# Mixers of a two-block model on one core: weight splits on VectorE, both base inverses in one pass, band attention paced anew, heads in the array's halves

## The chip, the cores and the metric

The kernel runs on one core of one Trainium2 chip, in one launch. The metric is the device time of the run in microseconds (us), the median of a few runs. The engines are TensorE (PE, with PEld for its weight loads), VectorE (DVE), ScalarE (ACT), GpSimd (POOL) and SyncE (SP), which here only issues transfers.

## The reference

Two blocks follow each other over 512 tokens of width 1024, all in float32. The first block has two layers, each a token mixing (a pooling branch, sparse attention with an index that picks 128 keys, memory attention) and a mixture of 16 experts. The second block is what the change is about: feed-forward, mixers, feed-forward.

```
proj = rms_norm(x) @ w_in                 # 1024 -> 3600
qkv_a, z_a, a_a, b_a, qkv_b = split(proj)
o_a = gdn_mixer(qkv_a, z_a, a_a, b_a)     # 4 heads of 128
o_b = dilated_mixer(qkv_b)                # 8 heads of 64
x = x + concat(o_a, o_b) @ w_out
```

`gdn_mixer` convolves q, k and v over five tokens, applies silu, normalises q and k, and runs a gated delta rule over the tokens in both directions: per block a lower (or upper) triangular system is solved (`tmat = inverse(1 + lmat)`), and a scan carries a state of 128x128 per head from block to block. `dilated_mixer` is softmax attention under a band mask with relative bias; its three dilations are merged in the kernel into one softmax whose bias has the logarithm of the number of patterns that hold a pair.

## The kernel before, in words

Everything on TensorE that is a dense product runs in three passes (`mm3`, `feat`, `tok`): each operand is split into a high half rounded to fp32r and the low rest, and high by high, high by low and low by high are summed. Smaller products run as plain fp32, which the trace shows as two records for each.

Weights come through one stream (`Stream`). `load` issues the transfers on SP's queue, `split` makes the high half on ScalarE (L182) and the low half by a subtraction (L185) on VectorE, or on GpSimd for the units that `plan` marks as slow; `SLOWP` marks ten of the twelve input panels of the mixers, 20 units. There are five staging places (`turn` takes the next); a panel gives its places back when it is done.

The order of the work is written out by a small planner. `Kern.now` is a clock of its own in nanoseconds. Dense products advance it by `adv`, and within the mixers' later part (`count`) every `mm` advances it by 214 or 4n/2.4 ns. Side tasks are generators that yield how long they want to pause; `run_tasks` and `drive` step the task that is due. All queues then run in the order so written. `pipeline` runs a list of items through stages with lags and pauses `gap` between: 4300 for the layers' attention, `self.gap` for the band attention.

The mixers (`mixers`) go as follows.

- Input panels: twelve panels `ga0..5` (for the delta rule, by `feat`) and `sq0..5` (for the band, by `tok`). Beside them run `conv` (five taps on VectorE at L1896 and L1898, tanh on ScalarE, transposes at L1915 and L1945, norms), `normed` (norms of the band's q and k, transposes at L1817), `gates` (decay sums, L1979 to L2013), `gdn_couples` (four couples of blocks: the strict triangle, stored to DRAM as `nd`, pauses `CP`), and `gdn_base` (the inverses of all 16x16 diagonal blocks by 15 steps of row updates on VectorE, L2092 and L2093, for one direction and then the other; stored to DRAM as `td`).
- `gdn_builds`: `load` fetches `dct` (8 transfers), `nd` (8) and `C` from `td` (4 for each direction) on SP's queue; `attend` makes the decayed products; three lanes of `invert` grow the 16x16 inverses to 128x128 with 64-column products. GpSimd spreads the base (L2172).
- `gdn_scan`: two chains, one for each direction, of four steps; then `close` and the output projection (`project`).
- `band_attention`: 32 items (8 heads by 4 query blocks) from the end of the panels on, interleaved with builds and scan by the planner; what is left runs after the scan. An item has a score (one fp32 product of 64 rows by 512 columns into a bank of tag `sa`), a softmax (L909 to L913), four transposes into a bank of tag `tp` (L864), a copy (L866), four value products over all 128 columns of a pair's values, of which the head's 64 are copied out (L1864).

The layers' sparse attention (`dsa`) uses the same `attention`; its scores already run in pairs: `pair` puts the two heads of a pair into the upper and lower 64 rows of the array, three fp32r passes each, from a query split by `halves`.

Of the kernel before, what the change touches and what calls it, by code (L numbers as in the profile page):

```python
# [18 lines left out]
NT = S // 128  # L19
# [213 lines left out]
class Kern:  # L233
# [218 lines left out]
    def plan(self):  # L452
# [49 lines left out]
        for j, (n, i) in enumerate(PANELS):  # L502
            c = (0 if n == "ga" else 2064) + i * 256
            ws.plan((n, i), W[:, c:c + 256], 8, 256, j in SLOWP)
# [287 lines left out]
    def halves(self, q):  # L792

        a = self.m1.tile([128, 2, 128], F32R, name="qs", tag="bt", bufs=2)
        self.split(a[:, 0], a[:, 1], q)
        return a

    def pair(self, q, kH, kL):
# [4 lines left out]
        for i, (a, b) in enumerate(((0, kH), (0, kL), (1, kH))):  # L803
            for r in range(2):
                c = slice(r * 64, r * 64 + 64)
                self.mm(ps[r], q[c, a, :], b[c], i == 0, i == 2)
        return ps

# [44 lines left out]
    def attention(self, pool, scores, v, add, width, out, tag="sa"):  # L853

        nc = self.nc

        def first(st, qb, h):
            st["P"] = self.softmax(scores(qb, h), add(qb, h), width(qb), pool)
# [19 lines left out]
    def dsa(self, qT, kH, kL, v, sc, oT, done):  # L878
# [3 lines left out]
        held, ready = {}, {}  # L882

        def split(i):
            if i < len(pairs):
                qb, pr = pairs[i]
                ready[i] = self.halves(qT[:, pr, qb * 128:(qb + 1) * 128])

        def scores(qb, h):
            if h % 2:  # L890
                split(qb * 4 + h // 2 + 1)
                return held.pop(h)
            pr, W = h // 2, (qb + 1) * 128
            ps, held[h + 1] = self.pair(ready.pop(qb * 4 + pr), kH[:, pr, :W], kL[pr // 2][:, pr % 2, :W])
            return ps

        def out(r, pr, c, po):
            self.split(oH[r, pr, c], oL[r, pr, c], po)
        split(0)
# [780 lines left out]
    def mixers(self, xT, close):  # L1680
# [13 lines left out]
        with ExitStack() as left:  # L1694
            pool = lambda n: left.enter_context(tc.tile_pool(name=n, bufs=1, reuse_waits="tile"))
            sw = pool("sw")
            qkv = [sw.tile([128, 4, S], F32, name=n) for n in ("sqT", "skT")]
            qkv.append(sw.tile([128, NT, 512], F32, name="sv"))
            with tc.tile_pool(name="cw", bufs=1, reuse_waits="tile", side="right") as cw:
                with tc.tile_pool(name="pn", bufs=1, reuse_waits="tile") as self.pn:  # L1700
                    self.za_panel(xT, 1)
                    tasks = [self.side(self.gates()), self.side(self.zgates())]
# [6 lines left out]
                with tc.tile_pool(name="bw", bufs=1, reuse_waits="tile", side="right") as self.bw:  # L1709
                    self.gap = G1  # L1710
# [8 lines left out]
            self.drive(lambda: att in self.tasks)  # L1719
        pool = lambda n: self.left.enter_context(tc.tile_pool(name=n, bufs=1, reuse_waits="tile"))  # L1720
# [68 lines left out]
    def windows(self, xT, qT, kT, v):  # L1789
# [8 lines left out]
        def normed(raw, dst, col):  # L1798
# [15 lines left out]
            for j in range(2):  # L1814
# [3 lines left out]
                nc.scalar.activation(dst[:, j, :], p, AF.Copy, scale=col)  # L1818
                yield 600

        def panel(i):
# [8 lines left out]
            if i < 4:  # L1830
                d = (qT if i < 2 else kT)[:, 2 * (i % 2):2 * (i % 2) + 2, :]
# [16 lines left out]
    def band_attention(self, at, qT, kT, v, oB):  # L1848
# [3 lines left out]
        def bias(h):  # L1852
            if h < 8:
                E[h] = at.tile([128, 896], F32, name="E", tag="E", bufs=2)
# [3 lines left out]
        def add(qb, h):  # L1858
            if qb == 0:
                bias(h + 1)  # L1860
            return E[h][:, 384 - 128 * qb:896 - 128 * qb]

        def out(r, pr, c, po):
            nc.vector.tensor_copy(oB[r, pr, c], po)  # L1864

        bias(0)
        def scores(qb, h):
            p0, pr = (h % 2) * 64, h // 2
            ps = self.psum("sa")
            self.mm(ps, qT[p0:p0 + 64, pr, qb * 128:(qb + 1) * 128], kT[p0:p0 + 64, pr, :], True, True)  # L1870
            return ps
        stages = self.attention(at, scores, v, add, lambda qb: 512, out)
        yield from self.pipeline([(qb, h) for h in range(8) for qb in range(NT)], stages, None)

    def gdn_in(self, xT):
# [6 lines left out]
        def conv(i, pss):  # L1882
# [138 lines left out]
    def gdn_couples(self, p):  # L2021
# [5 lines left out]
        bnd = p.tile([128, 2, 128], F32, name="bndN")  # L2027
# [42 lines left out]
        for d in range(2):  # L2070
            yield from self.gdn_base(p, d)
            self.based.append(d)

    def gdn_base(self, p, d):

        nc, V = self.nc, self.nc.vector
        B = p.tile([128, 16, 16], F32, name="B", tag="B")
        X = p.tile([128, 2, 16, 16], F32, name="X", tag="X")
        tmp = p.tile([128, 64], F32, name="Bt", tag="Bt")
        nc.sync.dma_start(B, bass.AP(tensor=self.nd.tensor, offset=self.nd.offset + d * 128 * STEP,  # L2080
                                     ap=[[STEP, 128], [128, 16], [1, 16]]))
        T = X[:, 0]
        Tf = T.rearrange("p r c -> p (r c)")
        nc.gpsimd.memset(Tf, 0.0)
        nc.gpsimd.memset(Tf[:, ::17], 1.0)
        yield 4000
        for k in range(15):
            j = 15 - k if d else k
            rows, cols = (slice(0, j), slice(j, 16)) if d else (slice(j + 1, 16), slice(0, j + 1))
            sh = [128, 15 - k, k + 1]  # L2090
            x = tmp[:, :sh[1] * sh[2]].rearrange("p (a b) -> p a b", b=sh[2])
# [287 lines left out]
```

## Time and profile before

| | us |
|---|---|
| median of 3 runs (lowest, highest) | 3046.87 (3046.29, 3047.41) |
| profiled execution, whole time | 3070.84 |
| its span, first to last instruction | 3069.1 |
| PE busy, PEld busy | 2840.8 (93%), 2274.0 (74%) |
| DVE, ACT, POOL busy | 1933.7 (63%), 1281.1 (42%), 495.7 (16%) |
| mean granted TensorE clock | 0.955 |

The profile is of one execution, and times within it count from the span's first instruction. Busy TensorE time is modelled and counts slow clock as busy; the granted clock is a share of full speed. A row with "[x <-engine tile line]" gives idle time before it and what ended that.

### The profile page before, as it was taken

What the parts mean: (1) busy time and instruction counts of PE and PEld (TensorE: products, weight loads), DVE (VectorE), ACT (ScalarE), POOL (GpSimd) and SP (SyncE); (2) the same over time, 40 slices, a digit from 0 to 9 for tenths busy, and PEclk for the clock granted to TensorE, in tenths of its full rate; (3) what the DMA queues carried; (4) which work ended last, traced back from release to release, by engine and by line L of the source; (5) the groups of instructions that cost most, each with busy time, mean ns of one, the idle gap of its engine ahead of it and who ended that gap; (6) DMA issues with size and microseconds to landing.
All of it is one profiled execution on the core that took longest, in us unless ns stands there. A gap on an engine that the chain in (4) does not pass through costs nothing. (4 is left out here: it accounts for less than half of the span.)

```text
span 3069.1 us, 38719 instructions
## 1 busy us (share of the span) xinstructions
PE 2840.8 (93%) x14283; PEld 2274.0 (74%) x14283; DVE 1933.7 (63%) x3555; ACT 1281.1 (42%) x2077; POOL 495.7 (16%) x546
## 2 busy tenths in 40 slices
PE   7989999999989898998899979999988698999998
PEld 7767778876757676876667757888877586787877
DVE  5677544798986876437799973333578546444244
ACT  3533432377864433422678832222334222323132
POOL 1000002264120000111551110000155121010000
PEclk9999989999989999998899989999999798999999
DMA  6212215899963122228799924323323401123231
GB/s 195 86 55 82 67 56 175 307 357 351 346 237 107 45 76 65 76 76 322 255 353 352 323 64 145 110 82 100 112 83 105 113 20 37 51 90 108 85 102 70
DMA packets 295586, 448.27 MB, mean 146 GB/s; under 512 B 30402, under 2 KB 155986, under 8 KB 294880
## 3 DMA queue, kind: packets, MB, share of 16 engines
q1 hardware_dynamic: 274816, 382.66, 37.8%
q0 software_dynamic: 20000, 60.99, 6.2%
q8 instruction: 114, 1.87, 0.2%
q10 hardware_dynamic: 576, 2.10, 0.2%
q14 instruction: 80, 0.66, 0.1%
HBM read 423.02 MB, written 34.65 MB: 149 GB/s over the span
## 5 line engine op out<-in xcount | busy, mean ns | idle before, releaser
L185 DVE TENSOR_TENSOR wL<-wR,wH 128x1024 fp32r<-128x1024 f32 (+2 forms) x361 | 445.1, 1256 | 259.5 <-ACT wH L182 257.2
L294 PE MATMUL mm<-xTH,wH 128*128 128x512 f32 (+1 forms) x1376 | 541.4, 393 | 0.3 <-ACT xTH L351 0.2
L294 PE MATMUL mm<-xTH,wL 128*128 128x512 f32 (+1 forms) x1376 | 531.2, 386 | 7.7 <-DVE wL L185 7.7
L294 PE MATMUL mm<-xTL,wH 128*128 128x512 f32 (+1 forms) x1376 | 529.6, 385 | 2.5 <-DVE xTL L352 2.5
L182 ACT CAST wH<-wR 128x1024 fp32r<-128x1024 f32 (+1 forms) x394 | 399.9, 1042 | 260.4 <-PE mm L294 222.3
L294 PEld LDWEIGHTS mm<-xTH,wL 128*128 128x128 f32 x1376 | 262.8, 191 | 66.5 <-DVE wL L185 15.1
L294 PEld LDWEIGHTS mm<-xTH,wH 128*128 128x128 f32 x1376 | 263.7, 192 | 55.0 <-issue 4.7
L294 PEld LDWEIGHTS mm<-xTL,wH 128*128 128x128 f32 x1376 | 263.6, 192 | 49.5 <-DVE xTL L352 3.2
L294 PE MATMUL mm<-wH,hH 128*128 128x512 f32 (+1 forms) x608 | 241.0, 396 | 0.0
L294 PE MATMUL mm<-wH,hL 128*128 128x512 f32 (+1 forms) x608 | 239.1, 393 | 0.6 <-DVE hL L352 0.6
L294 PE MATMUL mm<-wL,hH 128*128 128x512 f32 (+1 forms) x608 | 238.6, 392 | 0.0
L294 PE MATMUL mm<-wH,xTH 128*128 128x256 f32 (+3 forms) x576 | 203.6, 353 | 11.9 <-DVE rx L754 5.3
L294 PE MATMUL mm<-wH,gH 128*96 128x512 f32 x512 | 206.3, 403 | 0.0
L294 PE MATMUL mm<-wH,gL 128*96 128x512 f32 x512 | 203.6, 398 | 0.0
L294 PE MATMUL mm<-wL,gH 128*96 128x512 f32 x512 | 202.4, 395 | 0.0
L294 PE MATMUL mm<-wH,xTL 128*128 128x256 f32 (+3 forms) x576 | 190.6, 331 | 3.6 <-DVE xTL L352 3.6
L294 PE MATMUL mm<-wL,xTH 128*128 128x256 f32 (+3 forms) x576 | 190.1, 330 | 0.0
L185 DVE TENSOR_TENSOR wL<-wX,wH 128x1024 fp32r<-128x1024 f32 x142 | 169.2, 1222 | 7.3 <-ACT wH L182 6.9
L182 ACT CAST wH<-wX 128x1024 fp32r<-128x1024 f32 x142 | 145.3, 1049 | 9.6 <-PE mm L294 8.9
L1647 DVE TENSOR_TENSOR th<-th,mm 128x512 f32<-128x512 f32 x44 | 30.2, 687 | 168.8 <-PE mm L294 168.8
L294 PEld LDWEIGHTS mm<-wH,hL 128*128 128x128 f32 (+1 forms) x608 | 107.3, 177 | 34.0 <-DVE hL L352 1.4
L294 PEld LDWEIGHTS mm<-wH,xTH 128*128 128x128 f32 x576 | 113.4, 197 | 25.0 <-DVE rx L754 6.2
(529 smaller groups left out, 5316.2 us busy)
## 6 DMA issues: line engine op xcount, KB each, us to landing
wX<-in_w SPq DMA_DIRECT2D x141, 512.0 KB, 11.3
wR<-in_w_in SPq DMA_DIRECT2D x116, 512.0 KB, 3.7
wR<-in_w SPq DMA_DIRECT2D x73, 512.0 KB, 11.4
wY<-in_w SPq DMA_DIRECT2D x69, 512.0 KB, 10.7
X<-in_w SPq DMA_DIRECT2D x56, 512.0 KB, 11.9
wZ<-in_w SPq DMA_DIRECT2D x45, 512.0 KB, 10.7
wR<-in_ffn_w_gate SPq DMA_DIRECT2D x44, 512.0 KB, 3.9
wR<-in_ffn_w_up SPq DMA_DIRECT2D x44, 512.0 KB, 5.0
```

What stands on the lines that cost most here:

```text
L182: nc.scalar.copy(u.H[:, :n], u.R[:, :n])
L185: eng.tensor_tensor(u.L[:, :n], u.R[:, :n], u.H[:, :n].bitcast(F32), OP.subtract)
L294: self.nc.tensor.matmul(ps, a, b, start=start, stop=stop)
L1647: nc.vector.tensor_tensor(th, th, u, OP.mult)
```

## The change

- `SLOWP` goes: all weight splits of the mixers' panels subtract on VectorE. The first tap of the convolution becomes a scaled copy on ScalarE, issued at once for both halves of a panel.
- `gdn_base` handles both directions in one pass, its steps alternating between them; couples pause 1000 instead of 2000.
- The band's scores run as the layers' do, through `pair`: the keys are split into high and low when they are transposed (the low parts live in a staging place borrowed until the band attention ends, so four are left), the query by `halves`. Items go by pairs of heads.
- In `attention`, for band and layers, the value products of a pair run together in its odd item: each head has 64 stationary columns and writes its own 64 partitions of the bank; one copy or split takes out both. The band's bank for it has tag `tp` instead of `sa`.
- The pause of the band attention is 500 up to the first set of bases (`ready`), 2500 from there, 500 in the scan as before (it was 1500 up to the scan).
- Small: three bias tiles `E` instead of two, constants and squares in tiles that others had, two instead of three weight units split during the builds.

```diff
-G1, G2 = 1500, 500
+G0, G1, G2 = 500, 2500, 500
-CP = 2000
+CP = 1000
-SLOWP = range(2, 12)
+EB = 3
...
+    def beside(self, ps, a, b, start, stop):
+        self.nc.tensor.matmul(ps, a, b, start=start, stop=stop)
...
-            ws.plan((n, i), W[:, c:c + 256], 8, 256, j in SLOWP)
+            ws.plan((n, i), W[:, c:c + 256], 8, 256)
...
+    def paired(self, n, q, k, *pool):
+        state = []
+        def split(i):
+            return self.halves(q(i), *pool) if i < n else None
+        nxt = [0, split(0)]
+        def scores():
+            if not state:
+                state.extend(self.pair(nxt[1], *k(nxt[0])))
+                return state[0]
+            nxt[:] = [nxt[0] + 1, split(nxt[0] + 1)]
+            ps = state[1]
+            state.clear()
+            return ps
+        return scores
...
         def third(st, qb, h):
             n, pr = width(qb) // 128, h // 2
+            PT[h % 2] = st["PT"]
+            if h % 2 == 0:
+                return
             po = self.psum(tag, 128)
             for j in range(n):
-                self.mm(po, v[:, j, pr * 128:(pr + 1) * 128], st["PT"][:, j * 128:(j + 1) * 128], j == 0, j == n - 1)
-            r = slice((h % 2) * 64, (h % 2) * 64 + 64)
-            out(r, pr, slice(qb * 128, (qb + 1) * 128), po[r])
+                for r, mm in enumerate((self.mm, self.beside)):
+                    c = slice(pr * 128 + r * 64, pr * 128 + r * 64 + 64)
+                    mm(po[r * 64:r * 64 + 64], v[:, j, c], PT[r][:, j * 128:(j + 1) * 128], j == 0, j == n - 1)
+            out(pr, slice(qb * 128, (qb + 1) * 128), po)
...
+                    low, place = self.ws.borrow([128, 2, S], F32R, "skL")
+                    qkv[1].append(low)
...
-                    self.gap = G1
+                    self.gap = G0
...
-        stages = self.attention(at, scores, v, add, lambda qb: 512, out)
-        yield from self.pipeline([(qb, h) for h in range(8) for qb in range(NT)], stages, None)
+        items = [(qb, 2 * pr + r) for pr in range(4) for qb in range(NT) for r in range(2)]
+        scores = self.paired(16, lambda i: qT[:, i // 4, i % 4 * 128:(i % 4 + 1) * 128],
+                             lambda i: (kT[0][:, i // 4], kT[1][i // 8][:, i // 4 % 2]), at, "qs", 1)
+        stages = self.attention(at, scores, v, add, lambda qb: 512, out, "tp")
+        yield from self.pipeline(items, stages, None)
...
+            for f in range(2):
+                nc.scalar.activation(a[f], u[f][:, 0:S], AF.Copy, scale=cw[:, 2 * i + f, 0:1])
             for f in range(2):
                 c = 2 * i + f
                 yield 1200
-                V.tensor_scalar(a[f], u[f][:, 0:S], cw[:, c, 0:1], None, op0=OP.mult)
...
+        for d in range(2):
+            nc.sync.dma_start(Bs[:, d], bass.AP(tensor=self.nd.tensor, offset=self.nd.offset + d * 128 * STEP,
+                                                ap=[[STEP, 128], [128, 16], [1, 16]]))
...
         yield 4000
         for k in range(15):
+            part = []
+            for d in range(2):
...
+                V.tensor_tensor(x, Bs[:, d, rows, j:j + 1].to_broadcast(sh), T[:, j:j + 1, cols].to_broadcast(sh),
+                                OP.mult)
+                part.append((T[:, rows, cols], x))
+            for T, x in part:
+                V.tensor_tensor(T, T, x, OP.add)
             if k % 3 == 2:
                 yield 800
...
-        self.ws.limit += 3
+        self.ws.limit += 2
...
                 yield 3500
                 ready.add(d)
+                self.gap = G1
```

## Rows read from the trace of the kernel before

**Rows 1.** Windows: stretch, length, busy PE, PEld, DVE, ACT, POOL, clock, DMA.
```profile
2209.00:2402.00 193.00, 162.59 (x1013) 146.16 (x1012) 155.63 (x301) 73.28 (x132) 91.20 (x164) 0.92 0.34 93
2402.00:2430.00 28.00, 15.24 (x61) 11.06 (x60) 19.14 (x59) 12.92 (x35) 0.20 (x1) 0.70 0.82 224
2430.00:2527.00 97.00, 91.78 (x670) 78.46 (x671) 42.29 (x103) 24.12 (x59) 23.71 (x28) 0.89 0.05 16
2527.00:2592.00 65.00, 55.92 (x395) 46.68 (x393) 45.93 (x139) 18.17 (x49) 17.69 (x17) 0.97 0.10 31
2592.00:2640.00 48.00, 38.55 (x173) 26.06 (x173) 25.00 (x74) 20.59 (x55) 1.97 (x3) 0.77 0.19 65
```
**Rows 2.** Groups by line in the panels: count, busy us, mean ns, idle before.
```profile
L185 POOL TENSOR_TENSOR wL<-wR,wH 128x1024 fp32r<-128x1024 f32 x20 | 53.5, 2694 | 43.1 <-ACT wH L182 42.9
L1898 DVE SCALAR_TENSOR_TENSOR cu<-cu,cw 128x512 f32<-128x512 f32 x48 | 49.1, 1024 | 2.1
...
L1896 DVE TENSOR_SCALAR cu<-cu,cw 128x512 f32<-128x512 f32 x12 | 12.4, 1036 | 2.5 <-POOL cu L1890 2.5
```
**Rows 3.** Tile `cu` of the convolution: ns min/median/max, first and last start.
```profile
L1898 DVE SCALAR_TENSOR_TENSOR cu<-cu,cw x48: 742/752/2987, 2228.8 to 2385.0; 128x512 f32<-128x512 f32 x48
...
L1896 DVE TENSOR_SCALAR cu<-cu,cw x12: 473/480/2865, 2226.1 to 2382.0; 128x512 f32<-128x512 f32 x12
```
**Rows 4.** Waits in the panels: us in total, times, longest.
```profile
ACT sqr L1804 <- DVE sss L1806: 29.1, 4, 9.9
...
PE tp L1915 <- DVE cu L1907: 9.5, 3, 6.2
...
PE sa L2012 <- DVE Gc L2003: 7.4, 1, 7.4
```
**Rows 5.** Timeline of the tail, VectorE: start, us, operation.
```profile
2621.04 0.69 DVE L909 CUSTOM_DVE_ANT_0 P<-sa,E 128x512 f32<-128x512 f32 x1 [0.22 <-PE sa L294]
...
2623.62 0.69 DVE L909 CUSTOM_DVE_ANT_0 P<-sa,E 128x512 f32<-128x512 f32 x1
```
**Rows 6.** The page's costliest groups: weight splits on VectorE, whole span.
```profile
L185 DVE TENSOR_TENSOR wL<-wR,wH 128x1024 fp32r<-128x1024 f32 (+2 forms) x361 | 445.1, 1256 | 259.5 <-ACT wH L182 257.2
```
**Rows 7.** Tile `PT` in the second layer: value products.
```profile
L294 PE MATMUL mm<-PT,v x160: 270/275/583, 1099.5 to 1319.4; 128*128 128x128 f32 x160
```
**Rows 8.** Timeline of TensorE around one band head, at full clock.
```profile
2524.44 0.66 PE L864 MATMUL tp<-ident,P 128*128 128x128 f32 x4
2525.02 1.12 PE L294 MATMUL sa<-skT,sqT 64*128 64x512 f32 x2
2526.07 1.16 PE L294 MATMUL sa<-PT,sv 128*128 128x128 f32 x8
2527.07 1.06 PE L294 MATMUL mm<-vb,Tt 128*128 128x128 f32 x8
```
**Rows 9.** Timeline of TensorE around one pair of scores in a layer.
```profile
1295.23 0.50 PE L294 MATMUL sa<-kH,qs 64*128 64x512 f32 x2
1295.57 0.39 PE L294 MATMUL sa<-kL,qs 64*128 64x512 f32 x2
1295.80 0.40 PE L294 MATMUL sa<-kH,qs 64*128 64x512 f32 x2
1296.13 0.50 PE L294 MATMUL mm<-brH,wH 128*128 128x512 f32 x1
```
**Rows 10.** Timeline of the gap: SP's last loads, GpSimd's first use.
```profile
2423.19 5.72 SPq L2134 DMA_DIRECT2D C<-td  x4
...
2429.80 1.05 POOL L2172 TENSOR_TENSOR T<-C,blk 128x512 f32<-128x512 f32 x1 [30.17 <-DMA C<-td]
```
**Rows 11.** Windows of line L909 alone: the softmaxes within the inverses.
```profile
2430.00:2527.00 97.00, 7.30 (x21) 0.89 0.05 16
```
**Rows 12.** Timeline of weight loads in the inverses.
```profile
2451.52 1.83 PEld L294 LDWEIGHTS mm<-T,Z 128*128 128x128 f32 x8
...
2458.09 0.97 PEld L294 LDWEIGHTS mm<-Z,T 128*128 128x128 f32 x8
```

More of the change, by code (lines that the diff above doesn't have):

```diff
@@ L805, in pair @@
                 c = slice(r * 64, r * 64 + 64)
-                self.mm(ps[r], q[c, a, :], b[c], i == 0, i == 2)
-        return ps
+                self.nc.tensor.matmul(ps[r], q[c, a, :], b[c], start=i == 0, stop=i == 2)
+        if self.count:
+            self.now += 3 * W / 2.4
+        return ps
+    def paired(self, n, q, k, *pool):
[12 more added lines that the diff above has]
+        return scores
     def index(self, iqT, ikT, iw, sc, before, done):
@@ L853, in attention @@
     def attention(self, pool, scores, v, add, width, out, tag="sa"):
+        PT = {}
         nc = self.nc
         def first(st, qb, h):
-            st["P"] = self.softmax(scores(qb, h), add(qb, h), width(qb), pool)
+            st["P"] = self.softmax(scores(), add(qb, h), width(qb), pool)
         def second(st, qb, h):
@@ L881, in dsa, with out @@
         pairs = [(qb, pr) for qb in range(NT) for pr in range(4)]
[L882 to L899, printed above, removed]
+        def out(pr, c, po):
+            self.split(oH[:, pr, c], oL[:, pr, c], po)
+        scores = self.paired(16, lambda i: qT[:, pairs[i][1], pairs[i][0] * 128:(pairs[i][0] + 1) * 128],
+                             lambda i: (kH[:, pairs[i][1], :(pairs[i][0] + 1) * 128],
+                                        kL[pairs[i][1] // 2][:, pairs[i][1] % 2, :(pairs[i][0] + 1) * 128]))
         stages = self.attention(self.m1, scores, v, lambda qb, h: sc[qb], lambda qb: (qb + 1) * 128, out, "mm")
@@ L1719, in mixers @@
             self.drive(lambda: att in self.tasks)
+            self.ws.give_back(place)
         pool = lambda n: self.left.enter_context(tc.tile_pool(name=n, bufs=1, reuse_waits="tile"))
@@ L1858, in add, with out @@
         def add(qb, h):
-            if qb == 0:
-                bias(h + 1)
+            if qb == 0 and h % 2 == 0:
+                bias(h + 2)
+            elif qb == NT - 1 and h % 2:
+                bias(h + 2)
             return E[h][:, 384 - 128 * qb:896 - 128 * qb]
-        def out(r, pr, c, po):
-            nc.vector.tensor_copy(oB[r, pr, c], po)
+        def out(pr, c, po):
+            nc.vector.tensor_copy(oB[:, pr, c], po)
         bias(0)
[L1867 to L1871, printed above, removed]
-        stages = self.attention(at, scores, v, add, lambda qb: 512, out)
-        yield from self.pipeline([(qb, h) for h in range(8) for qb in range(NT)], stages, None)
+        bias(1)
+        items = [(qb, 2 * pr + r) for pr in range(4) for qb in range(NT) for r in range(2)]
[3 more added lines that the diff above has]
+        yield from self.pipeline(items, stages, None)
     def gdn_in(self, xT):
@@ L2069, in gdn_couples @@
             dec = ahead
-        for d in range(2):
[L2071 to L2085, printed above, removed]
+        yield from self.gdn_base(p)
@@ L2094, in gdn_base @@
+            for T, x in part:
+                V.tensor_tensor(T, T, x, OP.add)
             if k % 3 == 2:
                 yield 800
[L2096 to L2098 removed]
+        for d in range(2):
+            V.tensor_copy(Xs[d][:, 1], Xs[d][:, 0].rearrange("p r c -> p c r"))
+            for i in range(2):
+                nc.sync.dma_start(self.td[d, :, i], Xs[d][:, i].rearrange("p r c -> p (r c)"))
+            self.based.append(d)
```

46 lines of the change are left out of this document (27 added, 19 removed).

## The prediction

> **What bounds the kernel now.** I read the windows of the mixers first, then the groups of VectorE inside the first window, the waits, and single stretches of TensorE. The windows cut the mixers into five stages [rows 1]: the input panels from 2209 us, a loading gap, the inverses, the scan, and a tail of attention up to the output projection. The reader is to see that TensorE is busy 162.6 of 193 us in the panels, 15.2 of 28 in the gap, 91.8 of 97 in the inverses, 55.9 of 65 in the scan and 38.6 of 48 in the tail, and that its granted clock is under 1 in most of them.
>
> In the panels VectorE is the late engine: 155.6 of 193 us busy. Much of that is no work. The convolution's taps take 0.75 and 0.48 us in their median, yet average 1.02 and 1.04 us, up to 2.99 and 2.87 us [rows 2, 3]. In the same window GpSimd runs 20 weight subtractions of 2.69 us, 53.5 us in all [rows 2]; a stalled VectorE instruction lasts about as long as one of them. TensorE waits 9.5 us for a VectorE convolution result and 7.4 us for the gate sums from VectorE, and ScalarE waits 29.1 us for VectorE's sums of squares, behind which it gives back transposes late [rows 4].
>
> In the last three stages TensorE sets the pace of the inverses and, with the chain through VectorE, of the scan; the tail is band attention alone, at 2.6 us a head where the clock is full [rows 5].
>
> **The change part by part.**
>
> *Panels: splits from GpSimd to VectorE, first tap to ScalarE, bases in one pass, shorter pauses.* VectorE gains 20 splits of 1.26 us, 25.1 us [rows 6], and four low halves of the keys, for which I take the 0.69 us of another 128x512 read out of PSUM [rows 5], 2.8 us. It loses 12 first taps of 0.48 us, 5.8 us [rows 3], which go to ScalarE (even at 1 us each they fit beside its 73.3 busy of 193 us [rows 1]), and the stalls: 49.1 - 48 x 0.752 = 13.0 us and 12.4 - 12 x 0.480 = 6.6 us on the two groups of taps [rows 2, 3], 19.6 us (smaller groups add to it). So VectorE's 155.6 us changes by 25.1 + 2.8 - 5.8 - 19.6 = +2.5 us at worst on these rows, and by up to -20 us when the smaller stalled groups come along. A split also waits in VectorE's queue for ScalarE's cast: 259.5 us over 361 splits is 0.72 us each [rows 6], 14 us for 20, behind which gate and convolution steps queue. The two bases issue the same 60 small instructions, but in one pass, and with 16 pauses of 1 us less before them and one round of pauses (8 us) instead of two they end some 20 us sooner, away from the last convolutions, where the longest TensorE wait of 6.2 us lies [rows 4]. Their two loads and four stores on SP move with them and keep their order; SP's next work there is the gap's loads, which wait for the panels' end anyway. The borrowed staging place leaves four instead of five: one whole panel of two units ahead, where none of the listed TensorE waits was for a weight; its cost is nothing, and without that cover one split, 1.26 us, per panel.
> TensorE idles 193 - 162.6 = 30.4 us here. The bounds are no gain (VectorE stays full: it is then the bound) and 30 us. I take 20, nearer to the upper end, since the waits named above all go back to late VectorE work.
>
> *The layers.* The two heads' value products go side by side into 64-column halves. Layer attention now has 160 records of 128 columns in each layer [rows 7]; eight like them take 1.00 us up to the next product's start [rows 8], so 0.12 us a record, 19.2 us a layer. Side by side they take half: -9.6 us a layer, -19.2 us in both, the upper bound; nothing is the lower. Each entry into halves and out again costs something: the present pair of scores in row halves takes 0.90 us for three passes that at the middle one's 0.23 us would take 0.69 [rows 9], so 0.2 us a pair, 32 pairs, 6 us. Nothing hides this, as panels on the same TensorE queue follow: -13, and I take -12.
> No row here shows column halves. [...]
>
> *Gap.* Nothing in it gets shorter: the last loads for the inverses issue on SP at 2423 us and GpSimd starts the first at 2429.8 us [rows 10]. Taking two weight loads instead of three out of SP's way is worth 0.5 us at most. Level and bound constants now wait for the bases' tiles on GpSimd's queue, which were written long before: nothing. I take 0, with 3 us either way.
>
> *Band attention.* Now a head takes 2.63 us of TensorE: 0.58 transposes, 1.05 score, the rest values [rows 8]. A pair takes 5.26. Afterwards: transposes 1.16, scores 0.90 as in rows 9, values 1.0 with 0.2 for the halves: 3.2 us, or 2.1 us less per pair, 33 us over 16 pairs. VectorE trades a second output copy for a query split of like size.
> Where the pairs fall I add up from the planner's own charges (213 ns and more per product, pauses, gaps). Before, 4 heads start ahead of the first inverse, 10 during the inverses, 8 in the scan, 10 after; the trace has 21 records, two per head, in the inverses [rows 11]. Afterwards the first gap of 500 ns rules for only 3.5 us of planner's time, until the first set of bases is taken as ready; I add up 7, 9, 8 and 8. So attention is brought forward by 2 to 3 heads, not mostly.
> Inverses: 10.5 x 2.63 = 27.6 us of heads become 4.5 x 3.2 = 14.4, -13 us on an engine busy 95%; I take -12 (0 if the inverses' own chain takes over, -18 if the clock recovers sooner).
> Scan: 21.0 becomes 12.8, -8 us, of which I take -6, since VectorE's steps of the scan lie on the chain too and a pair holds both score banks until its second softmax, which scan products behind it in TensorE's queue must wait for: +5 to -12.
> Tail: two heads fewer at 2.6 us, -5 us, and a shorter stretch at the low clock; -9 (0 to -20). The staging place comes back only here; the projection's four units are split by then.
>
> *Sum:* 20 + 12 + 0 + 12 + 6 + 9 = 59 us. The profiled execution took 3070.84 us, so 3011.8; the median of the runs is 0.9922 of it, hence **2988 us**.
>
> **The rivals.** *Column halves do not overlap.* Then the layers give 0 and the value part of the band attention (0.8 us a pair, 13 us, of which I had counted 8) is lost too: -59 + 12 + 8 = -39, 3008 us. For it: no row has them. Against: row halves do overlap in rows 9 (six passes in 0.90 us).
> *The panels give nothing*, because splits on VectorE wait for casts (14 us) as long as the old stalls did. For it: VectorE's balance above is near zero on the rows named. Against: the largest stalls sit on instructions that TensorE waits for. -39 us, 3008 us.
> *Slower: TensorE falls to half clock (1.2 GHz) in the inverses and the scan.* From 2430 us the inverses' products ran at half rate though in queue one behind the other: eight weight loads took 1.83 us, and 0.97 us from 2458 on [rows 12]. The heads' wide scores, which the change thins out there, might be what brought the clock back. At full rate these two stages would hold 91.8 x 0.89 - 13 = 69 and 55.9 x 0.97 - 8 = 46 us; at half, 138 and 92 instead of my 85 and 59: +86 us, a net +27 and 3074 us. It decides once 59 us of full-rate work run at half rate, 118 of those 144 us. Against it: most of the inverses already run at full rate with the same products, and 97 us have a mean clock of 0.89 [rows 1].
> [...]
>
> **How the numbers follow.** Forecast 0.68, halves without overlap 0.14, panels without gain 0.10, half clock 0.06, no change because gains and new waits cancel 0.02. With the upper bounds of all terms (30 + 19 + 3 + 18 + 12 + 20 = 102 us) the time would be 2946; with both middle rivals at once (-19) 3028. The range is 2950 to 3030. A measurement of this kernel tells about 0.2%, 6 us, from no change. Faster 0.90, the same 0.04, slower 0.06.
>
> **What would show it.** Panels: VectorE's tap groups at 0.75 us in the mean, GpSimd without weight subtractions, the stage near 173 us. Layers: value products with 64 columns starting 0.06 us apart, or 0.12 if they do not overlap. Gap: first inverse still some 28 us after the panels. Inverses near 85, scan near 59, tail near 39 us. It is wrong if the panels do not shrink, if the half clock lasts past the first third of the inverses, or if waits of the scan for score banks appear.

## The result, and the profile after

The changed kernel takes 3086.5 us (median of four runs, 3086.2 to 3088.4). Against the kernel before, run beside it at 3046.3 to 3068.9 us, the ratio is 1.0114, 95% interval 1.0085 to 1.0143: slower, by about 1%. The prediction was 2988 us and faster.

Executions of one kernel here differ by 30 us and more, and the reason is the subject of this case: how early TensorE's clock comes back in the inverses. The profile behind [rows 1] is of an execution of 3071 us; of the 113 timed executions of that kernel 58 take 3043 to 3053 us and 31 take 3059 to 3079. In the other 24 it took 3102 to 3119 us, longer than the change, at a mean granted clock of 0.938 to 0.946 (0.960 to 0.966 in the shortest group); the ratios leave these out, and none was profiled.

The windows of the changed kernel by stage, panels, gap, inverses, scan and tail, answer to [rows 1]:

```profile
2206.00:2384.00 178.00, 157.34 (x1010) 142.03 (x1009) 130.62 (x313) 82.04 (x144) 45.16 (x145) 0.95 0.36 103
2384.00:2425.00 41.00, 23.10 (x132) 17.45 (x130) 27.67 (x77) 16.95 (x47) 7.78 (x9) 0.72 0.61 155
2425.00:2550.00 125.00, 118.59 (x658) 108.20 (x660) 38.43 (x100) 26.58 (x66) 19.69 (x23) 0.54 0.04 13
2550.00:2610.00 60.00, 46.77 (x363) 40.52 (x359) 37.16 (x120) 17.08 (x48) 12.93 (x14) 0.95 0.08 25
2610.00:2656.00 46.00, 28.02 (x185) 20.80 (x186) 27.05 (x79) 18.52 (x52) 1.30 (x2) 0.80 0.18 61
```

The panels fell from 193 to 178 us, the scan from 65 to 60, the tail from 48 to 46. The gap grew from 28 to 41 us, and the inverses from 97 to 125. In them the reader is to see the granted clock: 0.54 in the place of 0.89, with TensorE busy 118.6 of 125 us. At full clock that work would be 118.6 x 0.54 = 64 us, an estimate from these two numbers. At the low level, 0.50, a pass of 512 columns of the paired scores takes 0.43 us (2450.93 to 2451.36 us in the change, start to start), 0.23 at full clock [rows 9]: 1.2 columns per ns at 0.50, where the prediction and the expectations say 1.2 GHz.

To compare executions, the edges of the stages are taken from TensorE's records (last panel product, first and last inverse product, last scan product, first product of the projection). "Before" is the second profile, of an execution of 3052.6 us:

| us | before, 3052.6 | after, 3086.7 | difference |
|---|---|---|---|
| start of the mixers | 2181.7 | 2181.8 | +0.1 |
| panels | 217.7 | 203.1 | -14.6 |
| to the first inverse product | 29.7 | 32.0 | +2.3 |
| inverses | 81.0 | 127.3 | +46.3 |
| scan | 67.6 | 75.3 | +7.7 |
| tail | 44.7 | 36.9 | -7.8 |
| projection to the end | 430.2 | 430.4 | +0.2 |

The differences add up to 34.2 us, the two times differ by 34.1. One stage loses more than all others give.

**The panels** went as predicted. VectorE's groups of the panels, the four remaining taps and the weight splits, answer to [rows 2]:

```profile
L1923 DVE SCALAR_TENSOR_TENSOR cu<-cu,cw 128x512 f32<-128x512 f32 x48 | 36.4, 768 | 1.4
L185 DVE TENSOR_TENSOR wL<-wR,wH 128x1024 fp32r<-128x1024 f32 x22 | 26.6, 1220 | 21.9 <-ACT wH L182 21.9
```

The tap takes 0.768 us in the mean, down from 1.024; the splits wait 21.9 us for ScalarE's casts, the cost that was feared, and it does not eat the gain.

**The layers** went as predicted in mechanism only. One pair of heads' value products in the second layer, start and length of each record on TensorE, answers to [rows 7]:

```profile
1294.95 0.40 PE L294 MATMUL mm<-brH,wL 128*128 128x512 f32 x1
1295.28 0.32 PE L294 MATMUL mm<-PT,v 128*64 128x128 f32 x1
1295.29 0.32 PE L303 MATMUL mm<-PT,v 128*64 128x128 f32 x1
1295.44 0.27 PE L294 MATMUL mm<-PT,v 128*64 128x128 f32 x1
1295.45 0.27 PE L303 MATMUL mm<-PT,v 128*64 128x128 f32 x1
...
1296.09 0.27 PE L294 MATMUL mm<-PT,v 128*64 128x128 f32 x1
1296.10 0.27 PE L303 MATMUL mm<-PT,v 128*64 128x128 f32 x1
1296.30 0.50 PE L294 MATMUL mm<-brH,wH 128*128 128x512 f32 x1
1296.64 0.40 PE L294 MATMUL mm<-brL,wH 128*128 128x512 f32 x1
```

The two halves start 0.01 us apart, and a step of both follows every 0.105 us, no slower than one record after the other before (0.111 us, below). So they overlap. From the start of the product ahead to that of the second one behind are 1.69 us; without those two products' 0.23 us each the pair costs 1.22, of which 8 x 0.105 = 0.84 are steps and 0.38 are entry and exit. A single head in the same place, in the first profile of before:

```profile
1298.80 0.39 PE L294 MATMUL mm<-brH,wL 128*128 128x512 f32 x1
1299.03 1.05 PE L294 MATMUL mm<-PT,v 128*128 128x128 f32 x8
1299.84 0.48 PE L294 MATMUL mm<-brH,wH 128*128 128x512 f32 x1
1300.16 0.40 PE L294 MATMUL mm<-brL,wH 128*128 128x512 f32 x1
```

Reckoned in the same way it costs 0.90 us. Its eighth record starts at 1299.80 us, so a step takes 0.111 us, and eight of them are 0.89: next to nothing is left for entry and exit. A pair thus costs 1.22 us in place of 1.8, and the halves cost 0.38 us a pair where 0.2 was predicted. What the 0.38 us are spent on the trace does not show.

But in the first layer, groups of TensorE from 215 to 455 us, first of the kernel before, then of the change:

```profile
L294 PE MATMUL mm<-PT,v 128*128 128x128 f32 x160 | 27.1, 306 | 11.2 <-ACT PT L866 11.2
L864 PE MATMUL tp<-ident,P 128*128 128x128 f32 x80 | 15.4, 295 | 3.5 <-DVE P L913 3.5
```

```profile
L890 PE MATMUL tp<-ident,P 128*128 128x128 f32 x80 | 15.8, 302 | 16.1 <-DVE P L930 14.1 <-DVE pu L1005 2.0
L294 PE MATMUL mm<-PT,v 128*64 128x128 f32 x80 | 14.2, 313 | 0.0
L303 PE MATMUL mm<-PT,v 128*64 128x128 f32 x80 | 13.9, 312 | 0.1
```

The value products keep TensorE for 14 us instead of 27.1. The wait for PT (11.2 us) is gone, but the transposes now wait 14.1 us for the softmax, 3.5 before. The next two fences show one stretch of that layer, first with the change, then without it (the panels' part alone, below):

```profile
315.00:355.00 40.00, 32.63 (x136) 24.20 (x135) 22.71 (x57) 14.37 (x29) 0.00 (x0) 0.83 0.18 53
```

```profile
315.00:355.00 40.00, 32.75 (x152) 25.36 (x151) 24.30 (x63) 16.59 (x35) 0.00 (x0) 0.96 0.18 53
```

TensorE is busy for the same 32.6 and 32.75 of 40 us, with less work in it, and the clock is 0.83 in place of 0.96. In this stretch the 13 profiles with the changed layers show 0.83 to 0.91, the five without 0.96. The mixers start at 2179.4 us in the mean of the 13, at 2181.1 in that of the five (2174 to 2184 in all): 1.7 us of the 12 predicted, small beside the spread.

### The profile page after: what moved, and what is told of

The parts are those of the page before. It is cut to its first block, busy times and chain, and to the rows that moved or that the text cites. A ratio compares the mean times of both kernels' runs of the same rounds, so it can differ in the third digit from the quotient of the medians.

```text
span 3085.0 us, 38739 instructions
## 1 busy us (share of the span) xinstructions
PE 2847.3 (92%) x14315; PEld 2277.1 (74%) x14315; DVE 1897.2 (61%) x3535; ACT 1284.8 (42%) x2073; POOL 447.9 (15%) x526
## 5 line engine op out<-in xcount | busy, mean ns | idle before, releaser
L185 DVE TENSOR_TENSOR wL<-wR,wH 128x1024 fp32r<-128x1024 f32 (+2 forms) x381 | 470.1, 1256 | 277.6 <-ACT wH L182 268.5
L294 PEld LDWEIGHTS mm<-wH,hL 128*128 128x128 f32 (+1 forms) x608 | 107.3, 177 | 34.1 <-DVE hL L356 1.4
L294 PEld LDWEIGHTS mm<-wL,hH 128*128 128x128 f32 (+1 forms) x608 | 107.6, 177 | 30.4
```

The lines of the kernel that those rows point to most:

```text
L185: eng.tensor_tensor(u.L[:, :n], u.R[:, :n], u.H[:, :n].bitcast(F32), OP.subtract)
L294: self.nc.tensor.matmul(ps, a, b, start=start, stop=stop)
```

## The experiments

Each kernel ran beside the kernel before on one chip. "Early" means that the clock is back within the first 60 us or so of the inverses; a kernel's executions fall into groups by it. One execution of each kernel was profiled; the others are sorted by their time and their mean granted clock. All forms of attention below compute the same function.

**Four first cuts: forms, pace, panels.**

e1_forms puts the band attention's single-head forms back, the rest as changed:

```diff
-                    mm(po[r * 64:r * 64 + 64], v[:, j, c], PT[r][:, j * 128:(j + 1) * 128], ...)
+                self.mm(po, v[:, j, pr * 128:(pr + 1) * 128], st["PT"][:, j * 128:(j + 1) * 128], ...)
-        scores = self.paired(16, ...)
+            self.mm(ps, qT[p0:p0 + 64, pr, qb * 128:(qb + 1) * 128], kT[p0:p0 + 64, pr, :], True, True)
```

> The changed kernel with only its band attention put back to the single-head forms (one fp32 score of 512 columns, value products over all 128 columns, a head at a time; keys not split, so no staging place is borrowed); layers, panels, bases and pace as changed. Theory 'forms': TensorE stays at 1.2 GHz through the inverses since the paired forms are too short to bring the clock back; then here the granted clock returns within 40 us of the first inverse product, the stage takes 95 to 105 us at a mean clock over 0.8 instead of 125 us at 0.54, and the kernel takes about 3060 us (3050 to 3070) instead of 3086. Rival 'pace or start': the clock hangs on when and how thinly heads are issued (pauses of 2500 ns, or the emptier 40 us ahead); then it stays at 0.5 for most of the stage, the single forms cost some 1 us a head more at full clock and 2 at half, and the kernel takes 3095 to 3110 us.

Measured: ten executions, five at 3040.6 to 3049.0 us, five at 3072.2 to 3083.9, with a mean granted clock of 0.955 to 0.959 and of 0.943 to 0.947; ratio 1.0026 (0.998 to 1.0073). The profiled one, 3045.7 us, has full clock from 2426 us on and 86.1 us of inverses. Both theories are half right: the forms let the clock come back, but only in half of the executions.

e2_dense changes the pace alone:

```diff
-G0, G1, G2 = 500, 2500, 500
+G0, G1, G2 = 500, 500, 500
```

> The changed kernel with the heads paced by 500 ns instead of 2500 ns once the first bases are in: 18 heads are issued between the inverses instead of 9 (8 ahead instead of 5, 4 to 6 in the scan, none after). Theory 'forms': paired heads don't wake the clock however many they are; the inverses last 135 to 150 us at a clock near 0.5, the scan and the tail give back some 25 to 35 us, and the kernel stays within 10 us of 3086. Rival 'pace': denser heads bring the clock back in the first third of the inverses; the stage then takes 90 to 105 us with twice the heads, the tail falls away, and the kernel takes 3020 to 3045 us.

Measured: 3027.3 to 3030.8 us in four executions, ratio 0.9911 (0.9878 to 0.9943). With paired heads this dense the clock was early in all four. "Forms" alone falls. The first inverse product comes late all the same, at 2436 us; GpSimd's queue and then TensorE's show why:

```profile
2414.14 0.54 POOL L1878 DMA_DIRECT2D E<-brows  x1 [35.04 <-DVE st L926]
2419.72 0.54 POOL L1878 DMA_DIRECT2D E<-brows  x1 [5.04 <-DVE st L926]
2420.25 0.54 POOL L2201 MEMSET Z<- 128x512 f32 x1
2420.74 1.06 POOL L2205 TENSOR_TENSOR T<-C,blk 128x512 f32<-128x512 f32 x1
```

```profile
2427.99 0.43 PE L294 MATMUL tp<-PT,sv 128*64 128x128 f32 x2 [1.93 <-ACT PT L892]
2434.13 0.47 PE L303 MATMUL tp<-PT,sv 128*64 128x128 f32 x1 [5.70 <-ACT PT L892]
...
2436.02 1.97 PE L294 MATMUL mm<-Tt,NH 128*128 128x64 f32 x8
```

A bias load E waits for a softmax, and the T tiles stand behind it on GpSimd. TensorE has value products of a head ahead of the first inverse that wait 5.7 us for their PT.

e3_panels is the kernel before with the panels' part alone:

```diff
-CP = 2000
+CP = 1000
...
-SLOWP = range(2, 12)
+SLOWP = ()
...
+                nc.scalar.activation(a[f], u[f][:, 0:S], AF.Copy, scale=cw[:, 2 * i + f, 0:1])
...
-                V.tensor_scalar(a[f], u[f][:, 0:S], cw[:, c, 0:1], None, op0=OP.mult)
...
+        yield from self.gdn_base(p)
...
-            yield from self.gdn_base(p, d)
...
```

> The kernel before with the panels' part of the change alone: no weight subtractions on GpSimd, pauses of 1000 ns between couples, the first tap on ScalarE, the bases of both directions in one pass. Attention in layers and band as before. Theory: the panels shrink by 15 us as in the changed kernel (193 to 178 us) and the inverses keep the clock that they had, so 3047 - 15 = 3032 us (3025 to 3040). Rival 'earlier is colder': ending the panels earlier empties TensorE ahead of the inverses, the clock stays at 0.5 in them as in the changed kernel, and the kernel takes 3050 to 3075 us.

Measured: two executions at 3034.8 and 3037.2 us, eight at 3049.5 to 3056.5; ratio 0.9972 (0.9942 to 1.0002). The panels take 204.9 us between the edges of the table, 13 less than in the second profile of before. In the profiled execution (3050.6 us) the clock is back only at 2437 us and the inverses take 89.1 us, 8 more than in the second profile of before, and the tail 49.5, 5 more: so the 13 us go. Most executions lie at the lower edge of the rival's range, but its mechanism, half clock through the inverses, is not what the profile shows.

e4_pace is the kernel before with the change's pace:

```diff
-G1, G2 = 1500, 500
+G0, G1, G2 = 500, 2500, 500
...
-                    self.gap = G1
+                    self.gap = G0
...
+                self.gap = G1
```

> The kernel before with the pace of the change alone: pauses of 500 ns, then 2500 ns once the first bases are in, instead of 1500 ns throughout; 10 heads between the inverses instead of 9, 3 ahead in both. Theory 'forms': the clock comes back as before and the time stays within 6 us of 3047. Rival 'pace': with longer pauses the clock stays at 0.5 through the inverses and the kernel takes 3065 to 3085 us.

Measured: six of ten executions at 3054.3 to 3073.8 us, four at 3083.1 to 3085.1; ratio 1.0027 (0.9988 to 1.0065). The shortest execution lies 11 us above that of the kernel before beside it, but the interval does not exclude that nothing changed. The thin pace alone does not bind every execution.

**Is it the start, the pace or the form?**

> The changed kernel again, nothing altered, for the spread of its executions beside that of the kernel before (3043 to 3078 us in 24 executions). Theory: with paired heads 2500 ns apart the clock never comes back early in the inverses, so all executions lie within 5 us of 3086. Rival: the changed kernel too has an early and a late return of the clock and four executions happened to be late; then some of ten lie near 3050 us.

f1_again, the changed kernel: 3084.3 to 3093.6 us in four executions, mean granted clock 0.937 to 0.941, late in all by that, ratio 1.0116 (1.0073 to 1.0158).

f2_warm adds products of 512 columns ahead of each lane's first inverse product:

```diff
+                    self.sk = qkv[1][0]
...
+                if n < 3 and i == 4:
+                    ps = self.psum("mm")
+                    for _ in range(12):
+                        nc.tensor.matmul(ps, self.sk[:, 0, 0:128], self.sk[:, 0, :], start=True, stop=True)
```

> The changed kernel with 36 extra TensorE products of 512 columns over all 128 rows (their results are read by nobody), 12 ahead of the first inverse product of each of the three lanes; pace and forms as changed. Theory 'the clock has two stable levels here and the start decides': the extra products fill the wait at the start of the inverses, bring the clock to full, and the inverses then keep it by themselves; the stage falls from 125 to 75 to 90 us and the kernel takes 3035 to 3060 us. Rival 'the inverses themselves are too light': once the extra products are over the clock falls back to 1.2 GHz within 10 us, the extra work costs 8 to 15 us and the kernel takes 3090 to 3105 us.

Measured: four executions at 3045.4 to 3048.5, one at 3061.8, five at 3074.6 to 3078.5; ratio 1.0033 (0.9996 to 1.0071). Windows of the profiled one, 3078.5 us:

```profile
2440.00:2450.00 10.00, 10.00 (x95) 9.29 (x95) 3.57 (x10) 2.88 (x7) 0.00 (x0) 1.00 0.01 2
2450.00:2455.00 5.00, 3.68 (x43) 3.24 (x42) 2.30 (x6) 1.59 (x5) 3.26 (x5) 1.00 0.00 0
2455.00:2460.00 5.00, 5.00 (x34) 4.44 (x34) 1.65 (x4) 1.00 (x4) 2.01 (x2) 0.51 0.01 3
2460.00:2470.00 10.00, 10.00 (x49) 8.80 (x47) 2.53 (x7) 1.40 (x3) 2.55 (x3) 0.50 0.00 1
```

The third twelve of the extra products brought the clock to full (eight inverse products took 1.92 us ahead of them and 1.06 at 2440 us, behind), and 19 us after the last of them (2436.6 us) it fell again. TensorE's records around the fall:

```profile
2452.62 0.45 PE L294 MATMUL mm<-Tt,NH 64*64 64x64 f32 x5
2454.39 1.31 PE L294 MATMUL mm<-Tt,NH 128*128 128x64 f32 x8 [1.32 <-POOL Tt L2206]
2455.63 0.48 PE L294 MATMUL tp<-PT,sv 128*64 128x128 f32 x1
...
2457.53 1.33 PE L294 MATMUL mm<-Tt,NH 128*128 128x64 f32 x5
```

64x64 products of two lanes, then 1.3 us of waiting for GpSimd, then half clock. In three more profiles (f3_p1500 at 2484 us, e4_pace at 2513, h1_values at 2455) a fall inside the inverses follows a wait of 0.8 to 1.8 us too, with 64x64 products shortly ahead in f3_p1500 alone. Waits as long passed without a fall elsewhere: 1.84 us in g3_before (to 2433 us), 1.38 in i2_s1500 (to 2445). So such a wait does not decide it, and the inverses do not hold the level by themselves in every execution; the extra products help in half of them.

f3_p1500 gives the paired heads the pace of the kernel before:

```diff
-G0, G1, G2 = 500, 2500, 500
+G0, G1, G2 = 500, 1500, 500
```

> The changed kernel with the heads paced by 1500 ns, as in the kernel before, instead of 2500 ns once the first bases are in: 12 heads between the inverses instead of 9 (18 at 500 ns), 6 ahead. If the pace alone kept the clock down, the clock comes back within the first third as at 500 ns and the kernel takes 3030 to 3045 us; if the lightness of the paired heads counts as well, 1500 ns is not enough and it takes 3070 to 3090 us, in some executions at least.

Measured: six at 3039.3 to 3043.5 us, four at 3059.9 to 3064.1; ratio 0.9985 (0.9951 to 1.0019). Between the two, as a matter of degree.

f4_bdense gives the kernel before a denser pace:

```diff
-G1, G2 = 1500, 500
+G1, G2 = 500, 500
```

> The kernel before with its heads (single, heavy forms) paced by 500 ns instead of 1500 ns: 16 heads between the inverses instead of 9, 5 ahead. Theory 'pace': the clock returns early in every execution, the spread of the kernel before (3043 to 3078 us) closes to its lower end, and the shorter tail pays for the heads moved: 3030 to 3045 us. Rival 'the single forms gain nothing from it': the inverses grow by 7 heads of 2.6 us, 18 us, as much as the tail loses, with the old spread, 3045 to 3075 us.

Measured: seven at 3055.1 to 3064.9 us, three at 3080.8 to 3085.5; ratio 1.0042 (1.0001 to 1.0084), slower if anything. Its profile has full clock from 2441 us on, yet 106.1 us of inverses for a tail of 23.2: heavy heads moved in cost what the tail gives back. Here pace paid only with light heads.

**The gap, and a better pace.** g1_eact and g2_dense_eact move the bias loads:

```diff
-                nc.gpsimd.dma_start(E[h], ...)
+                nc.scalar.dma_start(E[h], ...)
```

> The changed kernel with its eight bias loads E issued from ScalarE's queue instead of GpSimd's, so that no bias load waiting for a softmax stands ahead of the inverses' first tiles T in GpSimd's queue (in the changed kernel the third lane's T waited 6.2 us behind one). If the late T counts for the 41 us gap, the first products of the inverses all start by 28 us after the panels and some 6 us are gained, 3080 us; the clock stays at 1.2 GHz in the inverses, since the pace is as it was. Rival: the same late start is what makes the clock fall, and with T in time it stays up: 3030 to 3050 us. No gain: 3086 us, if TensorE's queue and not GpSimd's holds the inverses up.

> The changed kernel paced by 500 ns, with the bias loads on ScalarE's queue. With the loads on GpSimd's queue the pace of 500 ns took 3030 us though its first inverse product came 20 us later than in the changed kernel (2436 against 2417), behind T tiles that waited for two bias loads (2414 to 2420) and behind eight heads in TensorE's queue. If GpSimd's queue is the larger part of this, 10 us or more are gained: 3015 to 3022 us. If the heads in TensorE's queue are, each pair of them a chain of some 12 us, under 4 us: 3026 to 3032 us.

Measured: g1 3087.5 to 3091.7 us (ratio 1.0127, 1.0078 to 1.0177); g2 nine at 3030.7 to 3033.9 and one at 3072.0 (0.9951, 0.9914 to 0.9989). In g1 GpSimd has the first lane's T at 2412.0 us and all three by 2417.1, and the first inverse product still comes at 2417.6 behind a pair of scores. No gain: the heads ahead in TensorE's own queue hold the inverses up.

g4_late2500 has that edit too, and turns the pauses round:

```diff
-G0, G1, G2 = 500, 2500, 500
+G0, G1, G2 = 2500, 500, 500
```

> The changed kernel with the pauses the other way round: 2500 ns ahead of the bases and 500 ns behind them, and the bias loads on ScalarE's queue. 5 heads stand ahead of the first inverse instead of 8 at 500 ns throughout, 17 between the inverses, 10 in the scan. Theory: the first inverse product comes at 2415 us as in the changed kernel, the heads behind it are dense enough that the clock comes back, and the kernel takes 3005 to 3020 us, the best so far. Rival: the clock comes back only because of the heads ahead; without them it stays at 1.2 GHz for 50 us or more and the kernel takes 3040 to 3080 us.

Measured: 3021.0 to 3024.1 us in all six executions, ratio 0.9896 (0.9854 to 0.9938). The best, 24 us under the usual 3047 of the kernel before and 64 under the change, though the first inverse product came at 2425 us and not at 2415.

> The kernel before, nothing altered, for a second profile of it: the first came from an execution of 3071 us, while most take 3044 to 3053 us. Expected: stages as before (panels 193, gap 30, scan 66, tail 49 us), and, if this execution is one of the short ones, inverses some 20 us shorter with TensorE at full clock nearly from their first product on.

g3_before, the kernel before: ten executions, eight at 3046.9 to 3076.8 us, two at 3108 and 3112; ratio to itself 1.004 (1.0003 to 1.0077). A ratio within 0.4% of 1 therefore tells nothing here, that of f4_bdense included. In the profiled one (3052.6 us) the clock is back at 2428 us, before the first inverse product, and the inverses take 81.0 us in place of 92.6. As expected.

Three kernels side by side, stretches of the inverses, first the change, then the kernel before (g3_before), then g4_late2500 (the inverses of the last two end at 2510 and 2508 us):

```profile
2430.00:2450.00 20.00, 20.00 (x103) 19.55 (x102) 4.54 (x14) 2.71 (x7) 0.57 (x1) 0.50 0.07 23
2470.00:2490.00 20.00, 20.00 (x96) 18.65 (x94) 3.58 (x10) 2.89 (x7) 2.55 (x3) 0.50 0.01 1
2510.00:2530.00 20.00, 20.00 (x111) 18.34 (x110) 5.21 (x16) 4.37 (x11) 4.38 (x5) 0.50 0.00 1
```

```profile
2430.00:2450.00 20.00, 18.16 (x147) 16.04 (x146) 10.67 (x24) 5.99 (x16) 4.63 (x6) 1.00 0.07 24
2470.00:2490.00 20.00, 20.00 (x176) 17.62 (x175) 8.11 (x23) 4.68 (x12) 2.55 (x3) 1.00 0.00 1
```

```profile
2430.00:2450.00 20.00, 20.00 (x190) 18.41 (x189) 9.83 (x29) 6.82 (x19) 0.00 (x0) 1.00 0.07 24
2470.00:2490.00 20.00, 19.24 (x196) 16.60 (x197) 10.65 (x31) 9.06 (x23) 5.10 (x6) 1.00 0.15 47
```

All have TensorE busy 18 to 20 of 20 us. The change puts 96 to 111 products into each stretch at 0.50, the kernel before 147 and 176 at 1.00, g4_late2500 190 and 196.

**Which form brings the clock back?** Five returns inside the inverses, in four profiles with single forms, came 0.5 to 1.6 us behind the end of a single head's value products. TensorE in e3_panels, full clock from 2437 us:

```profile
2431.38 1.91 PE L294 MATMUL mm<-T,Z 128*128 128x64 f32 x8
2433.09 1.92 PE L294 MATMUL mm<-Z,T 128*128 128x64 f32 x8
2434.80 2.02 PE L294 MATMUL sa<-PT,sv 128*128 128x128 f32 x8
2436.61 1.53 PE L294 MATMUL mm<-T,Z 128*128 128x64 f32 x8
2437.97 1.06 PE L294 MATMUL mm<-Z,T 128*128 128x64 f32 x8
```

Eight products over all 128 columns, 2.02 us at half clock, then inverse products that get faster within their group. That suggested the value products. Against it stand a sixth return with single forms (f4_bdense, 2441 us, 3.5 us behind the end of value products and amid transposes) and that of the change itself: its clock came back at 2535 us, while inverses still ran, at the end of a pair of scores (2533.7 to 2535.3 us). Of the diff of e1_forms, h1_values has the first two lines only (the value products), h2_scores the last two only (the scores), both at 2500. h1_values keeps the bank of tag `tp` (e1_forms goes back to `sa`) and the borrowed staging place; h2_scores, like e1_forms, does not split the keys and borrows none.

> The changed kernel, pace of 2500 ns as changed, with only the band attention's value products put back to one head at a time over all 128 columns; scores stay paired. In five profiles (the kernel before, the panels' part alone, the pace alone twice, the single forms) the clock came back 1 to 3 us behind a single head's eight value products. Theory 'value products': those are what brings the clock back, so some of the executions here have it back within 60 us of the first inverse product and lie at 3040 to 3060 us, the others at 3080 to 3090. Rival 'scores': the four-pass score of one head, 1.05 us against 0.9 us for a pair, is what counts; then all executions lie above 3080 us as with the change.

> The changed kernel, pace of 2500 ns as changed, with only the band attention's scores put back to one fp32 product of 512 columns per head (keys not split, no staging place borrowed); value products stay in column halves. Theory 'value products': the clock never comes back early, all executions lie at 3085 to 3105 us. Rival 'scores': some executions lie at 3040 to 3060 us as with both single forms (five of ten there).

Measured: h1_values ten executions between 3035.7 and 3069.8 us (ratio 1.002, 0.9985 to 1.0055), none at the 3086 of the change; the profiled one has the clock up from 2421 to 2455 us and again from 2500. h2_scores two at 3017.5 and 3028.6, two at 3087.1 and 3089.6 (no ratio). The theory of the value products falls: the scores alone do it too. Either heavier form is enough for some executions; only both light forms at the thin pace, with no products added, are late every time (after, f1_again and g1_eact, twelve executions).

i1_best and i2_s1500 keep the forms of h2 and change the pace, i1 with the bias loads on ScalarE:

```diff
-G0, G1, G2 = 500, 2500, 500
+G0, G1, G2 = 2500, 500, 500
...
-G0, G1, G2 = 500, 2500, 500
+G0, G1, G2 = 500, 1500, 500
```

> The scores of one head at a time (fp32) and value products in column halves, with pauses of 2500 ns ahead of the bases and 500 ns behind them and the bias loads on ScalarE's queue: 17 heads between the inverses instead of 9. At 2500 ns this form split into 3018 and 3029 us (clock up) and 3087 and 3090 us (clock down). Theory 'amount of head work between the inverses': all executions have the clock up early and lie within 10 us of each other, at 3005 to 3025 us. Rival 'chance at the start': the split stays, with some executions above 3060 us.

> The same forms with a pause of 1500 ns behind the bases, bias loads on GpSimd's queue as changed: 11 heads between the inverses. Theory 'amount of head work': fewer late executions than at 2500 ns (two of four), most at 3015 to 3035 us. Rival 'chance at the start': about half above 3060 us.

Measured: i1_best ten executions, 3025.1 to 3032.8 us, none late (0.9903, 0.9871 to 0.9936); i2_s1500 three at 3020.0 to 3023.3 and one at 3076.1 (0.9892 for the three, 0.9782 to 1.0001). With one form the early share goes with the amount of head work between the inverses: 9 heads split two and two, 11 three and one, 17 ten and none. Four executions each are few, so this is likely and not shown. Nor is head work a guarantee: f4_bdense with 16 heads had three long executions of ten and g2_dense_eact one; none of these was profiled.

## Why the prediction was wrong, point by point

**The failed step** is the price of the clock in the inverses. The sum took the stage at the clock of one profile and subtracted heads (-12), and gave the rival "half clock" 0.06 because "most of the inverses already run at full rate with the same products". The products were the same, but the clock there did not hang on them alone: it hung on the heads between them, which the change made lighter and set 2500 ns apart (0.50 in its stretches above, 1.00 in those of g4_late2500, whose light heads are 500 ns apart). The stage took 46.3 us more than in the second profile of before. The rival named the mechanism and its place, and its 3074 us was near; it expected half clock in the scan too, which ran at 0.95. The prediction's own sign of being wrong, half clock past the first third of the inverses, was met. It had also misread the half clock in the profile of before, as coming with a queue that was full: there TensorE waited 4.31 us for PT up to 2438.3 us, the clock fell at 2437.3, and only then was the queue full until the clock came back at 2457.8. That the stage stood on an edge could have been suspected from the runs: an execution of 3071 beside a median of 3047 hints that something in this kernel takes one of two levels.

**Waits and the clock.** In the change the gap ahead of the inverses, with TensorE busy 23.1 of 41 us, ran at 0.72, and the clock fell at 2422 us, one microsecond into a wait of 6.4 us. But waits do not account for what came after: from 2430 to 2530 us TensorE's records fill 99.8 of 100 us, and the clock stays at 0.50. The falls inside the inverses of other kernels do follow a wait (0.8 to 1.8 us), but waits of the same length passed without one (1.84 us in g3_before).

**Panels** -20 predicted, -14.6 measured: right, the size off by 5; the casts that splits wait for are part of it at most (21.9 us in place of 14 estimated).

**Layers** -12 predicted, -1.7 measured. The value products did halve. Entry and exit cost 0.38 us a pair and not 0.2, some 6 us over 32 pairs if all are like the one shown. The step that failed is that "panels on the same TensorE queue follow", so that freed time would count: the transposes wait for the softmax instead (14.1 us in the first layer, 3.5 before), and the clock dips (0.83 in the stretch shown, 0.96 without the change).

**Gap** 0 predicted, +2.3 to the first inverse product. By the windows it is 13 us longer: the first inverse product comes at 2416.8 us, but TensorE then waits from 2421.3 to 2427.7 us, 6.4 us, for ScalarE's Z.

**Scan** -6 predicted, +7.7 from the last inverse to the last scan product (its start still runs at the low clock, 0.72 from 2550 to 2560), -5 by the windows. **Tail** -9 predicted, -7.8 measured, -2 by the windows: right in direction.

**Brought forward**: 5 heads stand ahead of the first inverse product in TensorE's order, 9 more up to the last one (3 and 9 before). The planner's sum said 7 and 9.

**What stays open**: why one and the same kernel falls on either side of the edge, and what exactly of a head counts. With the value products alone or the scores alone in their old form the clock came back early in some executions, so no single form can be named. Nor is it shown what the kernel before does in its executions of 3102 to 3119 us. If its clock is late there throughout the inverses, the change, late in all twelve executions at 3084 to 3094 us, is the shorter of the two in the like case, and loses because it made the late case the rule.

## What to carry to other kernels

Making filler work lighter beside a stage of small products can cost more than it frees: here the heads decided how often TensorE ran the stage at full clock (1.00, and 0.50 with the change). Where a kernel's executions fall into two groups, profile one of each before costing a change; the sum must say on which side it lands. If light filler is wanted, issue it densely inside the weak stage and not ahead of it: that order, with the bias loads moved (which alone gave nothing), turned 3086 into 3023 us. Most of it is the density: 500 ns throughout took 3030.

## What was not expected of the hardware

A TensorE whose records leave next to no idle time can stay at half clock for 100 us (2430 to 2530 us, 99.8 us busy, 0.50 throughout, 529 products), while the same stage with more heads in it runs at full clock (g4_late2500, 1.00 from 2425 to 2508 us with 776 products). Twelve products of 512 columns over all rows, three times, raised it in the profiled execution of f2_warm (1.00 from 2440 to 2455 us), and it fell again 19 us after the last of them. Entering and leaving column halves costs 0.38 us for eight steps of 0.105, where eight products over all columns show no such cost (0.90 us, of which eight steps of 0.111).
